# A hybrid decoder trunk: columns of layer 1's modulation on VectorE, head 1's queries and keys in the gates' banks, sums of activations behind the last exchange of banks

## The chip, the cores and the metric

The kernel runs on one core of one Trainium2 chip. The time is that of the device, in microseconds, from the start of the program to its end. Three runs of the kernel before gave 2206.76, 2210.25 and 2211.48; the median is 2210.25. A core has five engines that follow their own queues of instructions and wait for each other by semaphores: TensorE (PE: matrix products; its loads of weights are shown apart, as PEld), VectorE (DVE), ScalarE (ACT), GpSimd (POOL) and SyncE (SP), which here only issues transfers. Transfers between the large memory and the core's own memory are made by 16 DMA engines.

## The reference, cut to what matters

Two layers work on 512 tokens of width 2048 in 32-bit floats. The first is a multi-scale retention with 8 heads, the second a latent attention with 16 heads. Ahead of each, the activations are normalised and modulated by a conditioning vector c:

```python
c_act = jax.nn.silu(c)
for i in range(DEPTH):
    mod = (c_act @ ada_w[i] + ada_b[i])[:, None, :]
    shift, scale, gate = jnp.split(mod, 3, axis=-1)
    h = rmsnorm(x, norm_g[i]) * (1.0 + scale) + shift
    ...
    y = retention_branch(h, positions, ret_w_in[j], ret_gn_g[j], ret_w_out[j])
    ...
    x = x + gate * y
return rmsnorm(x, final_norm_g)
```

The retention branch first makes `h @ w_in`, which holds queries and keys, values and gates of all heads; then it turns queries and keys by the positions (rope), forms the retention per head, normalises, multiplies by `silu(g)` and goes through `w_out`. The change touches only the modulation of the first layer (called layer 1 in the title; index 0 in the code) and the projection `h @ w_in` for heads 0 and 1.

## The kernel before

**Numbers in two parts.** Each 32-bit operand of a product is split into a high part and a low part in TensorE's own rounded format (`split`, L135 and L136: ScalarE casts the high part, VectorE subtracts it to get the low one), and each product is made as three: high by high, high by low, low by high. A tile of h, `hT[kt]`, holds 128 of the 2048 features for all 512 tokens, high and low.

**The first stage: head 0 while h is made.** h is not complete when the kernel starts. Its 16 k-tiles are made two at a time (a unit `u` is the tiles 2u and 2u+1), and each unit is multiplied with head 0's weights as soon as it is there. For each tile two rows of the modulation are needed, the shift and the scale. `sum_mod` (L355) forms each as a sum over 2048 products on VectorE, in place on a loaded tile `aw` of 1 MB, and leaves one number per partition, `mc`. `make_first` (L365) turns the two into the column `b_col` (shift plus bias) and the column `a_col` ((scale + bias) times the gain of the norm), with two instructions on 128x1 elements on POOL (L368, L369). `make_h` (L243, L245) then makes h on ScalarE, once rounded as the high part and once in full as `h_<kt>f`, and VectorE subtracts the two for the low part (L246). The `aw` tiles have four buffers, which is one unit's worth.

Head 0 has three sets of four results: queries and keys (`qk`), values (`v`) and gates (`g`). The accumulator memory has eight banks, four under the tag `acc` and four under `aux`. The gates keep `aux` for the whole stage. `qk` and `v` share `acc` in turn: `swap` copies the four banks of one out to ordinary memory (L381) and those of the other back in (L385), pair by pair, on ScalarE. In unit u one of the two is `here` and one `there`; the products of a unit come in the order here, gates, exchange, there, and the next unit's `here` is the same kind, so that one exchange per unit is enough. `prepare_ahead(u + 1)` puts the work for the next unit ahead of these products: the split of the new `here` weights, the sums of the modulation, the normalisation of the next x tiles (`xT`, L541), h of tile 2u+2, and the splits of gate and `there` weights. `prepare_behind` puts h of tile 2u+3 behind the exchange.

**The end of the stage.** In the last unit, behind h of tile 15, two of eight groups of sums of activations are formed (`form_sums`, L441 to L446 and the split of their results; they are operands of the seven-product scheme that the later heads use for values and gates), then the tables of cosines and sines (`rotary_tables`, L257 to L280: a load of the positions on ScalarE's queue, 17 steps on VectorE, two on ScalarE). The last products of `here` and of the gates follow; then the values are copied out and stored (POOL issues the stores), `qk` comes back for its last 24 products, and the tables are stored.

**Head 1 and on.** The work of the later heads is a list of steps; each step loads weights three ahead, splits them one step ahead and multiplies. Head h makes its queries and keys in 8 steps of 24 products into four `acc` banks (L161 to L163), then values and gates in 16 steps by seven products instead of eight (L745 to L747), into x and s (banks `acc`) and z and y (banks `aux`). Between the stage above and the first step stands the evacuation of head 0: four copies of `qk` (`keep_rows`, L653) and four of the gates with Silu, each followed by a store that POOL issues. The remaining six groups of sums are formed in the first steps of head 1.

**What sets the order.** `queued` and `behind` fix the order per engine: what is emitted under them comes, on ScalarE, VectorE, TensorE and SP, behind the last instruction emitted there so far. An engine works through its queue in order. POOL is not among these four; its instructions come in the order of the scheduler. Tiles come from rings of buffers (six for `tmp`, from which h in full, the positions, the copies on their way to a store and the sums all take one), and a tile waits until the buffer that it takes is free.

Of the kernel before, what the change touches and what calls it, by code (L numbers as in the profile page):

```python
# [12 lines left out]
AF = mybir.ActivationFunctionType  # L13
ALU = mybir.AluOpType
AX = mybir.AxisListType

P = 128
# [32 lines left out]
def hybrid_trunk_kernel(  # L50
# [26 lines left out]
    PE, ACT, DVE, POOL = nc.tensor, nc.scalar, nc.vector, nc.gpsimd  # L77
# [11 lines left out]
    g_d = dram.tile([RH * T, T], F32, name="g_d")  # L89
# [5 lines left out]
    def big(name, dt=F32R):  # L95
        return base.tile([P, 2, T], dt, tag="big", bufs=16, name=name)
# [7 lines left out]
    def tmp(name, shape=(P, T)):  # L104
        return base.tile(list(shape), F32, tag="tmp", bufs=6, name=name)
# [95 lines left out]
    def w_block(w, ki, b):  # L201
        return w[0][:, ki, b * P : (b + 1) * P], w[1][:, ki, b * P : (b + 1) * P]
# [4 lines left out]
    def act_row(t):  # L207
        return t[:, 0, :], t[:, 1, :]
# [8 lines left out]
    bias_c = (vcol[:, 0:32], vcol[:, 32:64])  # L217
    norm_c = (vcol[:, 64:80], vcol[:, 80:96])
# [5 lines left out]
    a_col = [base.tile([P, KD], F32, name=f"a_col{i}") for i in range(2)]  # L224
    b_col = [base.tile([P, KD], F32, name=f"b_col{i}") for i in range(2)]
# [14 lines left out]
    def make_h(i, kt, src, dst):  # L240

        sc, bi = a_col[i][:, kt : kt + 1], b_col[i][:, kt : kt + 1]
        ACT.activation(dst[:, 0, :], src, AF.Identity, bias=bi, scale=sc)  # L243
        hf = tmp(f"h{i}_{kt}f")
        ACT.activation(hf, src, AF.Identity, bias=bi, scale=sc)  # L245
        return lambda: DVE.tensor_sub(dst[:, 1, :], hf, dst[:, 0, :].bitcast(F32))  # L246
# [51 lines left out]
    def qk_parts(h, u):  # L298
        return [
            (lambda raw: raw[:, :, 0:256], rows(w_ret_in, u, 2, h * 256, 256)),  # L300
            (lambda raw: raw[:, :, 256:512], rows(w_ret_in, u, 2, 2048 + h * 256, 256)),
        ]

    hT = [None] * KD
# [10 lines left out]
    banks = {}  # L315
# [31 lines left out]
    mods = {}  # L347
# [17 lines left out]
    def make_first(kt):  # L365

        k1 = slice(kt, kt + 1)
        POOL.tensor_add(b_col[0][:, k1], mods[kt, 0], bias_c[0][:, k1])  # L368
        POOL.tensor_scalar(  # L369
            out=a_col[0][:, k1], in0=mods[kt, 1], scalar1=bias1[:, k1], scalar2=norm_c[0][:, k1], op0=ALU.add, op1=ALU.mult  # L370
        )
        hT[kt] = big(f"hT_{kt}")
        return make_h(0, kt, xT[kt // 2][:, kt % 2, :], hT[kt])
# [38 lines left out]
    @contextmanager  # L412
    def behind(*engines):

        with ExitStack() as stack:
            for e in engines:
                ins = next((i for i in reversed(nc.cur_bb.bb.instructions) if i.engine == e), None)
                if ins is not None:
                    stack.enter_context(tc.issue_after(ins))
            yield  # L420

    def queued(fn, *args):
        with behind(A_, V_, T_, S_):
            return fn(*args)
# [59 lines left out]
    bias1 = l0p.tile([P, KD], F32, name="bias1")  # L484
# [58 lines left out]
    def load_unit(u):  # L543
        here, there = ("qk", "v") if u % 2 == 0 else ("v", "qk")
        load_first(here, u)
        load_mods(2 * u)
        if u > 1:
            queued(nc.sync.dma_start, xT[u], x_t[u])
        load_first("g", u)
        mods[2 * u + 1, 0] = queued(load_mod, 2 * u + 1, 0)  # L550
        load_first(there, u)
        mods[2 * u + 1, 1] = queued(load_mod, 2 * u + 1, 1)

    late = {}
    sums1 = {}
# [5 lines left out]
    def prepare_ahead(u, first=None):  # L561


        here, there = ("qk", "v") if u % 2 == 0 else ("v", "qk")
        low = queued(prepares[here, u])
        queued(sum_mod, 2 * u, 0)
        if first is not None:
            queued(first)
        queued(low)
        if u > 1:  # L570
            queued(normalise, u)
        queued(sum_mod, 2 * u, 1)
        low = queued(make_first, 2 * u)
        queued(sum_mod, 2 * u + 1, 0)
        queued(low)
        low = queued(prepares["g", u])
        late[u] = queued(prepares[there, u])
        queued(low)
        queued(sum_mod, 2 * u + 1, 1)

    def prepare_behind(u):

        low = queued(make_first, 2 * u + 1)
        queued(late[u])
        return low
# [26 lines left out]
    for u in range(1, NU):  # L612

        here, there = ("qk", "v") if u % 2 == 0 else ("v", "qk")
        more = u + 1 < NU
        if more:
            load_unit(u + 1)
            prepare_ahead(u + 1, low)
        else:
            queued(low)  # L620
            for n in range(2):
                queued(form_sums, n, hT, sums1, staged0, None)
            for _ in range(8):
                queued(next, tables)
        for kt in (2 * u, 2 * u + 1):
            queued(products, here, kt)
        for kt in (2 * u, 2 * u + 1):
            queued(products, "g", kt)
        if more:
            queued(swap, here, there)  # L630
            low = prepare_behind(u + 1)
        else:
            for b, ps in enumerate(banks["v"]):
                st = tmp(f"v0_st{b}")
                queued(ACT.copy, st, ps)
                POOL.dma_start(v_d[b * P : (b + 1) * P, :], st)
            queued(swap, None, "qk")
            for _ in tables:
                pass
            for n, t in enumerate(ret_tables):  # L640
                POOL.dma_start(tables_d[n * P : (n + 1) * P, :], t)
        queued(bank_products, there, u)
    qk0, g0 = banks["qk"], banks["g"]
    l0.__exit__(None, None, None)


# [215 lines left out]
    def qk_parts_of(h):  # L862
        return lambda u: qk_parts(h, u)
# [5 lines left out]
    for h in range(1, RH):  # L869
        if h < 6:  # L870
            steps += plain_steps(
                8, 2, qk_parts_of(h), 512, f"qk{h}", acc, 4,
                lambda w, ki, kt, b: w_block(w, ki, b), lambda w, ki, kt, b: act_row(hT[kt]),
                lambda b, ps, h=h: keep_rows(ps, qk_d, (4 * h + b) * P, f"qk{h}_st{b}", own=in_turn(b)),
                rows=lambda u, h=h: int(h > 1),
                sums=lambda u, h=h: {0: 2, 1: 3, 3: 4, 4: 5, 6: 6, 7: 7}.get(u) if h == 1 else None,
            )
        steps += heads_steps(h)
# [235 lines left out]
    for h in (6, 7):  # L1114
# [3 lines left out]
            lambda b, ps, h=h: keep_rows(  # L1118
                ps, qk_d, (4 * h + b) * P, f"qk{h}_st{b}",
                own=tmp,  # L1120
            ),
# [785 lines left out]
    n_prepared = prepare_for(0)  # L1907
    for b in range(4):
        queued(keep_rows, qk0[b], qk_d, b * P, f"qk0_st{b}", AF.Identity, in_turn(b))
    for b in range(4):  # L1910
        queued(keep_rows, g0[b], g_d, b * P, f"g0_st{b}", AF.Silu, tmp)
    for i, step in enumerate(steps):
        if i == n_p:
            lp.__exit__(None, None, None)
# [271 lines left out]
```

## Time and profile before

| what | value |
|---|---|
| median of three runs | 2210.25 us (2206.76 to 2211.48) |
| the profiled execution's own time | 2210.5 us |
| its span, first to last instruction | 2208.7 us |
| mean granted clock of TensorE | 0.992 |
| instructions | 27660 |
| busy share PE, DVE, ACT, POOL | 98%, 71%, 46%, 6% |
| chain of waits, by engine | PE 80%, DVE 8%, issue 4%, ACT 3%, DMA 3%, POOL 1% |
| moved from and to the large memory | 443.41 MB, 201 GB/s in the mean |

The profile records one execution. Start times count from the start of the span. A row of a group or of a timeline gives the line of the kernel, the engine, the operation, the tile written and the tiles read, and at its end in brackets the idle time of the engine ahead of it and what ended that. The chain of waits is followed back from the last instruction of a stretch: at each step to what released it. "issue" is time in it for which the profile shows no cause. A window sums busy time per engine between two instants and gives the granted clock (1.00 is full speed), the share of the DMA engines and the rate. TensorE's products overlap, so that busy time counts a little more than their spacing.

### The profile page before, as it was taken

How to read it: one execution, taken by the hardware profiler on the slowest of the kernel's cores; microseconds unless marked ns; L12 is line 12 of the kernel's file. 1: busy time of each engine (PE TensorE's matmuls, PEld its weight loads, DVE VectorE, ACT ScalarE, POOL GpSimd, SP SyncE). 2: the span in 40 equal slices, each digit the busy share in tenths (PEclk: the TensorE clock that was granted, in tenths of full speed). 3: DMA queues.
4: the chain of work that ended last, by engine and by line, in shares of the span. 5: the costliest groups of instructions: out<-in, count | busy, mean ns of one | idle time of the engine just before them, and what ended most of it. 6: DMA issues, size and time to landing. Idle time of an engine off the chain costs nothing.

```text
span 2208.7 us, 27660 instructions
## 1 busy us (share of the span) xinstructions
PE 2159.7 (98%) x10192; PEld 1802.5 (82%) x10192; DVE 1560.8 (71%) x2317; ACT 1006.0 (46%) x1516; POOL 140.7 (6%) x210
## 2 busy tenths in 40 slices
PE   7888999999999999999999999999999999999997
PEld 5777888888888877888888888888888888898887
DVE  7777866767675798866676776658877667776545
ACT  5554443434343444434343535434444266664443
POOL 1321000000100000000000000000000000000000
PEclk9999999999999999999999999999999999999999
DMA  9974686676867688673555556444457733235333
GB/s 382 358 257 147 191 281 224 225 257 195 280 200 267 209 281 270 219 242 127 208 201 166 203 164 219 157 157 129 143 196 281 286 96 94 77 114 172 119 105 133
DMA packets 205691, 443.41 MB, mean 201 GB/s; under 512 B 19393, under 2 KB 56289, under 8 KB 201713
## 3 DMA queue, kind: packets, MB, share of 16 engines
q1 hardware_dynamic: 193344, 402.45, 54.6%
q0 software_dynamic: 11920, 38.91, 4.5%
q8 instruction: 80, 1.31, 0.3%
q14 instruction: 57, 0.47, 0.1%
q10 hardware_dynamic: 290, 0.27, 0.0%
HBM read 398.56 MB, written 43.00 MB: 200 GB/s over the span
## 4 chain that ended last, share of the span: by engine, by line
PE 80%; DVE 8%; issue 4%; ACT 3%; DMA 3%; POOL 1%; SPq 0%; DVEq 0%; POOLq 0%; ACTq 0%
PE o L1196 13%; PE qk L161 4%; PE qk L162 4%; PE qk L163 4%; PE o L2052 4%; PE x L746 2%; PE y L746 2%; PE y L747 2%; PE y L745 2%; PE x L747 2%; PE s L746 2%; PE s L747 2%; PE x L745 2%; PE s L745 2%; PE o L163 2%
## 5 line engine op out<-in xcount | busy, mean ns | idle before, releaser
L1196 PE MATMUL o<-o_h,o_whi 128*128 128x512 f32 (+1 forms) x496 | 192.2, 388 | 0.0
L1196 PE MATMUL o<-o_h,o_wlo 128*128 128x512 f32 (+1 forms) x496 | 191.4, 386 | 0.0
L1196 PE MATMUL o<-o_l,o_whi 128*128 128x512 f32 (+1 forms) x496 | 191.3, 386 | 0.0
L161 PE MATMUL qk<-hT,qk_h 128*128 128x512 f32 x448 | 175.7, 392 | 5.7 <-ACT qk_st L653 5.7
L162 PE MATMUL qk<-hT,qk_h 128*128 128x512 f32 x448 | 175.3, 391 | 0.0
L163 PE MATMUL qk<-hT,qk_l 128*128 128x512 f32 x448 | 175.3, 391 | 0.0
L136 DVE TENSOR_TENSOR o_wlo<-o_r,o_whi 128x1024 fp32r<-128x1024 f32 x61 | 74.6, 1223 | 80.9 <-ACT o_whi L135 80.9
L136 DVE TENSOR_TENSOR qk_l<-qk_r,qk_h 128x1024 fp32r<-128x1024 f32 x56 | 68.1, 1223 | 68.5 <-ACT qk_h L135 68.2
L1196 PEld LDWEIGHTS o<-o_h,o_wlo 128*128 128x128 f32 x496 | 93.2, 188 | 18.9
L1196 PEld LDWEIGHTS o<-o_h,o_whi 128*128 128x128 f32 x496 | 93.2, 188 | 18.2
L1196 PEld LDWEIGHTS o<-o_l,o_whi 128*128 128x128 f32 x496 | 93.2, 188 | 18.2
L161 PEld LDWEIGHTS qk<-hT,qk_h 128*128 128x128 f32 x448 | 84.8, 189 | 23.7 <-ACT qk_st L653 6.1
L163 PEld LDWEIGHTS qk<-hT,qk_l 128*128 128x128 f32 x448 | 84.6, 189 | 17.9 <-DVE qk_l L136 0.3
L162 PEld LDWEIGHTS qk<-hT,qk_h 128*128 128x128 f32 x448 | 84.7, 189 | 17.6
L135 ACT CAST qk_h<-qk_r 128x1024 fp32r<-128x1024 f32 x56 | 57.9, 1050 | 85.9 <-PE qk L162 66.5
L898 DVE SCALAR_TENSOR_TENSOR mod<-mod,c_bm 128x1024 f32<-128x1024 f32 x64 | 78.0, 1219 | 20.5 <-DMA mod<-in_ada_t_dram 20.5
L161 PE MATMUL g<-h,g_h 128*128 128x512 f32 x232 | 90.6, 390 | 0.3 <-ACT g_h L135 0.3
L162 PE MATMUL g<-h,g_h 128*128 128x512 f32 x232 | 90.3, 389 | 0.0
L163 PE MATMUL g<-h,g_l 128*128 128x512 f32 x232 | 89.8, 389 | 0.0
L355 DVE SCALAR_TENSOR_TENSOR aw<-aw,c_all 128x2048 f32<-128x2048 f32 (+1 forms) x34 | 72.9, 2160 | 3.6 <-DMA aw<-in_ada_t_dram 3.1
L135 ACT CAST o_whi<-o_r 128x1024 fp32r<-128x1024 f32 x61 | 63.5, 1052 | 20.2 <-issue 10.0
L136 DVE TENSOR_TENSOR o_w_lo<-o_w_raw,o_w_hi 128x1024 fp32r<-128x1024 f32 x32 | 39.0, 1220 | 36.9 <-ACT o_w_hi L135 36.8
(1259 smaller groups left out, 6039.8 us busy)
## 6 DMA issues: line engine op xcount, KB each, us to landing
mod<-in_ada_t_dram SPq DMA_DIRECT2D x128, 512.0 KB, 6.0
o_r<-in_ret_w_out_dram SPq DMA_DIRECT2D x64, 512.0 KB, 4.3
aw<-in_ada_t_dram SPq DMA_DIRECT2D x30, 1024.0 KB, 8.8
qk_r<-in_ret_w_in_dram SPq DMA_DIRECT2D x112, 256.0 KB, 4.1
g_r<-in_mla_w_in_dram SPq DMA_DIRECT2D x32, 512.0 KB, 4.6
o_w_raw<-in_mla_w_out_dram SPq DMA_DIRECT2D x32, 512.0 KB, 3.7
qk_d<-qk_st POOLq DMA_DIRECT2D x32, 256.0 KB, 3.5
qk_r<-qk_d SPq DMA_DIRECT2D x32, 256.0 KB, 5.9
```

The source lines that it names most:

```text
L135: ACT.copy(hi, src)
L136: DVE.tensor_sub(lo, src, hi.bitcast(F32))
L161: PE.matmul(o, lhs[0], rhs[0], start=first and not seeded, stop=False, skip_group_check=seeded)
L162: PE.matmul(o, lhs[0], rhs[1], start=False, stop=False, skip_group_check=seeded)
L163: return PE.matmul(o, lhs[1], rhs[0], start=False, stop=last, skip_group_check=seeded)
L355: DVE.scalar_tensor_tensor(out=aw[:, cols], in0=aw[:, cols], scalar=1.0, in1=c_all[:, cols], op0=ALU.mult, op1=ALU.mult, accum_out=col[:, ...
L745: PE.matmul(banks[b], a[0], w[0], start=first, stop=False, skip_group_check=True)
L746: PE.matmul(banks[b], a[0], w[1], start=False, stop=False, skip_group_check=True)
L747: PE.matmul(banks[b], a[1], w[0], start=False, stop=True, skip_group_check=True)
L898: DVE.scalar_tensor_tensor(out=aw, in0=aw, scalar=1.0, in1=silu_c[j], op0=ALU.mult, op1=ALU.mult, accum_out=mc[:, j, b : b + 1],)
L1196: PE.matmul(o, w[i][:, ki, c0 + b * P : c0 + (b + 1) * P], a[j], start=first and i + j == 0, stop=last and i == 1, skip_group_check=True,)
L2052: PE.matmul(banks2[b][:, cols], w[0][i][:, 0, b * P : (b + 1) * P], o2_moving(w, u, cols)[j], start=u + i + j == 0, stop=u == KD - 1 and i ...
```

## The change

It has three parts. The two columns of `make_first` are formed on VectorE: the addition stays an addition, and the other becomes one instruction with two inputs and a scalar. Head 1's queries and keys take the `aux` banks, which the gates of head 0 held, instead of `acc`. And at the end of the first stage the order is another: the first two groups of sums move from behind h of tile 15 to behind the last exchange of banks and the tables; the gates of head 0 are copied out and stored there, ahead of the sums, instead of behind the queries and keys of head 0.

```diff
@@ make_first
-        POOL.tensor_add(b_col[0][:, k1], mods[kt, 0], bias_c[0][:, k1])
-        POOL.tensor_scalar(
-            out=a_col[0][:, k1], in0=mods[kt, 1], scalar1=bias1[:, k1], scalar2=norm_c[0][:, k1], op0=ALU.add, op1=ALU.mult
+        DVE.tensor_add(b_col[0][:, k1], mods[kt, 0], bias_c[0][:, k1])
+        DVE.scalar_tensor_tensor(
+            out=a_col[0][:, k1], in0=mods[kt, 1], scalar=bias1[:, k1], in1=norm_c[0][:, k1], op0=ALU.add, op1=ALU.mult
         )
@@ the last unit, behind h of tile 15
             queued(low)
-            for n in range(2):
-                queued(form_sums, n, hT, sums1, staged0, None)
             for _ in range(8):
                 queued(next, tables)
@@ the last unit, behind the exchange
             for n, t in enumerate(ret_tables):
                 POOL.dma_start(tables_d[n * P : (n + 1) * P, :], t)
+            for b, ps in enumerate(banks["g"]):
+                st = tmp(f"g0_st{b}")
+                queued(ACT.activation, st, ps, AF.Silu)
+                POOL.dma_start(g_d[b * P : (b + 1) * P, :], st)
+            for n in range(2):
+                queued(form_sums, n, hT, sums1, staged0, None)
         queued(bank_products, there, u)
-    qk0, g0 = banks["qk"], banks["g"]
+    qk0 = banks["qk"]
@@ the steps of queries and keys
-                8, 2, qk_parts_of(h), 512, f"qk{h}", acc, 4,
+                8, 2, qk_parts_of(h), 512, f"qk{h}", aux if h == 1 else acc, 4,
@@ ahead of the loop over the steps
     for b in range(4):
         queued(keep_rows, qk0[b], qk_d, b * P, f"qk0_st{b}", AF.Identity, in_turn(b))
-    for b in range(4):
-        queued(keep_rows, g0[b], g_d, b * P, f"g0_st{b}", AF.Silu, tmp)
```

Three places show how instructions move. The first is VectorE in the middle of the first stage, around h of tile 8 (`aw_0` and `aw_1` are the loaded rows of shift and scale, `mc` their sums; lines with + are new):

```order
 L541 TENSOR_TENSOR xT_209<-xT_209,x_factors 128x1024
 L355 SCALAR_TENSOR_TENSOR aw_1_720,mc_1_739<-aw_1_720,c_all 128x2048
+L368 TENSOR_TENSOR b_col_90<-mc_0_734,vcol 128x1
+L369 SCALAR_TENSOR_TENSOR a_col_88<-mc_1_739,bias_140,vcol 128x1
 L355 SCALAR_TENSOR_TENSOR aw_0_725,mc_0_747<-aw_0_725,c_all 128x2048
 L246 TENSOR_TENSOR hT_743<-h_8f,hT_743 128x512
 L334 TENSOR_TENSOR g_4_k4b_751<-g_4_raw,g_4_k4b_750 128x1024
 L355 SCALAR_TENSOR_TENSOR aw_1_729,mc_1_757<-aw_1_729,c_all 128x2048
+L368 TENSOR_TENSOR b_col_90<-mc_0_747,vcol 128x1
+L369 SCALAR_TENSOR_TENSOR a_col_88<-mc_1_757,bias_140,vcol 128x1
 L334 TENSOR_TENSOR v_4_wlo_754<-v_4_raw,v_4_whi_753 128x1024
```

Each pair now stands in VectorE's queue right behind the second of its two sums; POOL's queue loses the same 32 instructions.

The second is ScalarE from h of tile 15 to the first weights of head 1, before (`qk_0_h` is the high part of head 1's first weights, `qk_24_0` a bank of head 0's queries and keys, `g_0` one of its gates):

```order
L245 ACTIVATE h_15f<-xT_212,b_col_90,a_col_88 128x512
L135 CAST sums_1281<-sums_f 128x2x256
...
L254 DMA ret_pi<-in_positions_dram 128x512
...
L279 ACTIVATE ret_sin<-ret_sin 128x512
L280 ACTIVATE ret_cos<-ret_cos,rt 128x512
L135 CAST qk_0_h<-qk_0_r 128x1024
L653 ACTIVATE qk_st_1435<-qk_24_0_1381 128x512
...
L653 ACTIVATE g_st_1447<-g_0_305 128x512
```

The same with the change:

```order
L245 ACTIVATE h_15f<-xT_212,b_col_90,a_col_88 128x512
L254 DMA ret_pi<-in_positions_dram 128x512
...
L279 ACTIVATE ret_sin<-ret_sin 128x512
L280 ACTIVATE ret_cos<-ret_cos,rt 128x512
L424 ACTIVATE g_st_1363<-g_0_305 128x512
...
L135 CAST sums_1384<-sums_f 128x2x256
...
L135 CAST qk_0_h<-qk_0_r 128x1024
L657 ACTIVATE qk_st_1447<-qk_24_0_1351 128x512
```

The load of the positions follows h at once; four gate copies and four casts of sums now stand ahead of the cast of head 1's weights. On VectorE the sums stand likewise between the last step of the tables and the low part of these weights.

The third is TensorE where head 1's queries and keys end and its values and gates begin, before:

```order
L163 MATMUL qk_3_1469<-hT_1242,qk_7_l 128x512
L745 MATMUL z_0_1842<-vg_00o_h,hT_335 128x512
L746 MATMUL z_0_1842<-vg_00o_l,hT_335 128x512
L747 MATMUL z_0_1842<-vg_00o_h,hT_335 128x512
L745 MATMUL x_0_1838<-vg_00e_h,hT_271 128x512
```

and with the change:

```order
L163 MATMUL qk_3_1469<-hT_1242,qk_7_l 128x512
L749 MATMUL x_0_1838<-vg_00e_h,hT_271 128x512
L750 MATMUL x_0_1838<-vg_00e_l,hT_271 128x512
L751 MATMUL x_0_1838<-vg_00e_h,hT_271 128x512
L749 MATMUL x_1_1839<-vg_00e_h,hT_271 128x512
```

The first three products of z (a bank that was free while queries and keys held `acc`) no longer come first; x and s do, whose banks are now free.

## The prediction

> **What bounds the kernel now.** I read the page first (shares, slices), then the chain of waits, then windows cut at the places where the chain shows a repeat, and last the timelines of single engines inside one repeat.
>
> ```profile
> PE 2159.7 (98%) x10192; PEld 1802.5 (82%) x10192; DVE 1560.8 (71%) x2317; ACT 1006.0 (46%) x1516; POOL 140.7 (6%) x210
> ```
>
> TensorE is busy for 98% of the span, so little can be won by faster work elsewhere, except where TensorE is idle or slow. One such stretch is the first 190 us, which the change touches. There each unit of two k-tiles costs 72 products: 24 of queries and keys, 24 of values, 24 of gates. I cut the windows at the first product behind each exchange of banks; the columns are time, busy time and instruction count of PE, PEld, DVE, ACT, POOL, granted clock, DMA share, GB/s.
>
> ```profile
> 44.41:62.84 18.43, 15.61 (x60) 11.96 (x60) 15.89 (x15) 10.46 (x16) 4.46 (x4) 0.91 1.02 411
> 62.84:81.80 18.96, 16.62 (x73) 13.44 (x73) 14.95 (x15) 10.49 (x16) 5.98 (x4) 1.00 1.00 381
> 81.80:101.89 20.09, 18.26 (x73) 14.59 (x73) 14.95 (x15) 10.59 (x16) 5.97 (x4) 0.92 0.83 321
> 101.89:121.96 20.07, 18.24 (x73) 14.59 (x73) 14.95 (x15) 10.59 (x16) 5.98 (x4) 0.91 0.86 307
> 121.96:140.91 18.95, 16.63 (x72) 13.43 (x73) 14.95 (x15) 10.47 (x16) 5.98 (x4) 1.00 0.89 338
> 140.91:160.93 20.02, 18.20 (x72) 14.62 (x72) 14.95 (x15) 10.59 (x16) 5.97 (x4) 0.92 0.52 187
> 178.99:190.30 11.31, 5.61 (x26) 4.32 (x24) 8.66 (x15) 2.67 (x4) 1.08 (x2) 0.93 0.11 42
> 200.00:220.00 20.00, 20.00 (x90) 16.57 (x89) 18.34 (x31) 8.94 (x13) 0.00 (x0) 1.00 0.48 151
> ```
>
> The five full repeats last 19.0 to 20.1 us. No engine fills one: TensorE has 16.6 us of work at full clock, VectorE 14.95, ScalarE 10.5. So a loop of dependences sets the period, and the chain of waits spells it out for the repeat that ran at clock 1.00 (start, length, what):
>
> ```profile
> 121.03 2.30 DVE aw L355 x2
> ...
> 123.43 3.38 POOL a_col L369
> ...
> 127.55 0.80 ACT h_11f L245
> 128.35 0.95 ACT qk_whi L332
> ...
> 130.47 1.22 DVE xT L541
> 131.69 2.22 DVE aw L355 x2
> ...
> 134.00 2.32 POOL a_col L369
> ...
> 137.07 0.80 ACT h_12f L245
> 137.88 0.94 ACT g_k4b L332
> 138.81 0.94 ACT v_whi L332
> ...
> 140.27 0.60 ACT qk L385
> ...
> 140.91 0.79 PE qk L398
> ```
>
> POOL's 128x1 operation stands in that loop twice, for 5.7 of 18.95 us. Its length is not its work. The timelines of POOL and VectorE show one beside an idle VectorE and one beside a busy one:
>
> ```profile
> 32.83 0.34 POOL L369 TENSOR_SCALAR a_col<-mc,bias,vcol 128x1 f32<-128x1 f32 x1 [4.54 <-DVE aw L355]
> 94.79 2.29 DVE L355 SCALAR_TENSOR_TENSOR aw<-aw,c_all 128x2048 f32<-128x2048 f32 x1
> 94.98 2.31 POOL L369 TENSOR_SCALAR a_col<-mc,bias,vcol 128x1 f32<-128x1 f32 x1 [8.20 <-DVE aw L355]
> ...
> 55.79 2.46 POOL L369 TENSOR_SCALAR a_col<-mc,bias,vcol 128x1 f32<-128x1 f32 x1 [4.54 <-DVE aw L355]
> ```
>
> The first took 0.34 us alone; the second 2.31 us, with a long sum on VectorE, ending just behind it. POOL gets its turn only when VectorE's next instruction is over, and ScalarE's h waits for that.
>
> **Part 1, the columns on VectorE.** 32 small POOL instructions go, 32 come on VectorE, each pair right behind the sum that it needs. Nearest row for their length, and the row that tells what else holds ScalarE at the odd tile:
>
> ```profile
> 21.15 0.16 DVE L361 TENSOR_TENSOR mc_0b<-mc 128x1 f32<-128x1 f32 x1
> 125.04 0.59 ACT L385 COPY v<-part_v 128x512 f32<-128x512 f32 x1
> ```
>
> One costs 0.16 us; a pair, overlapped as neighbours on VectorE are, about 0.3 until ScalarE may start. Even tile: the sum ends at 133.91, so h starts at 134.3 where POOL let it start at 136.35: 2.05 us. Odd tile: ScalarE itself is in the exchange until 125.63, so h starts there instead of 126.83: 1.2 us. The loop falls from 18.95 to 15.7. VectorE gains two pairs, some 0.4 us of its own time: 15.4 of work. They wait for nothing but the sum in front of them; what stands behind them there (the next sum, or the low half of the other kind's weights) moves by 0.2 us. Even if a small instruction cost double, 0.32, the loop would be 16.0.
>
> TensorE's 72 products are then the longest: 16.4 us (16.63 busy counts the fill of the last product twice; 72 at the spacing of the last window, 20.00 us for some 88, give 16.4). So the period becomes 16.4, TensorE does not wait for an exchange, and with no gap I take the clock as 1.00, as in 200 to 220. The bounds of a period are 16.3 and 20.1, today's.
>
> Loads must keep up: a unit moves 338 GB/s x 18.95 us = 6.4 MB (307 x 20.07 gives 6.2); at 6.3 MB, the 411 GB/s of the first window needs 15.3 us, the 338 of a later one 18.6. I take 411: there the engines were full (1.02), later they had nothing asked of them (0.89).
>
> ```profile
> aw<-in_ada_t_dram SPq DMA_DIRECT2D x18, 1024.0 KB, 7.8
> ```
>
> A column load lands 7.8 us after its issue; in a 16.4 us period the sum that frees a buffer lies 11 us or more ahead of the next use.
>
> Up to the first of these windows the loads are late and little changes. The exchange at its end follows h of tile 4, whose column took 2.46 us on POOL (the row at 55.79) and should take 0.3: the product at 62.84 comes at 60.7. Five periods of 16.4 put the product now at 160.93 to 142.7: **18.2 us gained**, the main term.
>
> **Part 2, the order behind the last tile.** The chain of waits of this place, then single rows that price the moved work:
>
> ```profile
> 165.35 0.72 ACT h_15f L245
> ...
> 173.93 3.20 DMA ret_pi<-in_positions_dram
> ...
> 186.85 0.70 DVE ret_cos L277
> ...
> 188.82 0.93 ACT qk_h L135
> ...
> 190.30 0.79 PE qk L161
> ```
>
> ```profile
> 166.70 1.29 DVE L441 TENSOR_TENSOR h_f<-hT 128x512 f32<-128x512 f32 x2
> 171.01 1.28 DVE L441 TENSOR_TENSOR h_f<-hT 128x512 f32<-128x512 f32 x2
> 193.24 2.09 ACT L653 ACTIVATE g_st<-g 128x512 f32<-128x512 f32 x4
> 189.11 0.54 POOL L641 DMA_DIRECT2D tables_d<-ret_cos  x1
> v_d<-v_st POOLq DMA_DIRECT2D x4, 256.0 KB, 3.2
> ```
>
> From the end of h_15f (166.05) to the first product of head 1 (190.30) are 24.25 us, of which TensorE is idle for the last 5.7. Two sums of 4.31 us each came first, and the load of the positions, on ScalarE's queue, was issued behind their casts. Now this load is issued right behind h_15f, the tables follow, and the sums come behind them, ahead of the split of head 1's first weights on both engines. SP's queue keeps its order.
>
> With h_15f ending at 147.7 (5.0 behind 142.7; it was 5.12 behind 160.93, with a POOL wait of 1.2 partly in it): load 3.2, tables 10.4 (177.13 to 187.55), so the tables end at T = 161.4. ScalarE then has sine and cosine (1.27, from 187.55 to 188.82) and four gates (2.0): it is free for casts at T+3.3, some 0.7 later than the first sums could use it, so these end at T+5.0. The second sums take the buffer of a gate: its copy ends at T+1.8, POOL's issues (three of 0.54, two for the tables) end at T+2.65, landing near T+5.5 at 3.2 us. They take 4.31, and their last cast ends some 0.8 before their last low half: T+9.05; head 1's high part ends at T+10.0, the first product runs at T+10.05 = 171.5. Its low part follows 1.3 us later, which costs the third product 0.25 us. From h_15f to there are 24.05 us: **0.2 us gained**, a draw. TensorE's stall stays, about 7 us where it was 5.7, because what it waits for moved from the emptying of head 0's banks to the sums. If the store lands only after 7.8 us, like the column loads, the part costs 4.6 more; if it never matters, 0.5 less.
>
> **Part 3, head 1 in the gates' banks.** The four gate copies move ahead of head 1 (priced above, they lie beside the sums on VectorE). At the end of head 1's queries and keys, x and s no longer wait for ScalarE:
>
> ```profile
> 236.84 0.39 PE L747 MATMUL z<-vg_00o_h,hT 128*128 128x512 f32 x1
> 237.33 0.50 PE L745 MATMUL x<-vg_00e_h,hT 128*128 128x512 f32 x1
> ```
>
> Products are 0.23 apart, so 0.26 us was lost; z and y, which wait now, come 2.8 us later, behind the copies. **0.26 us gained.** On POOL's queue the four gate stores pass the four of head 0's queries and keys, 0.54 us each; the only one of these that anything here waits for is priced above.
>
> **Sum.** 18.2 + 0.1 (offset of h_15f) + 0.2 + 0.26 = 18.8 us. The profiled execution took 2210.5 (span 2208.7), 0.25 above the median of the runs: 2210.5 - 18.8 = 2191.7. Behind 260 us TensorE is never idle for long and no stage is tied to the clock on the wall, so the gain stays.
>
> **Rivals.** *The clock keeps falling.* In four of six windows the clock was 0.91 or 0.92 and the same products took 18.2 us. If gaps are not the cause, the period is 18.2: the last exchange comes at 60.7 + 91 = 151.7, gain 9.2 + 0.6, time 2200.7. Against it: 1.00 in 200 to 220, where TensorE never waits. The Trainium skill, "TensorE: Matmul & The Clock Gate", section "What's actually happening", has the clock halve after an idle window of about 3.4 us. By that rule the gaps here (18.95 less 16.63, so 2.3) are too short to halve it, and this rival would hold; the rows leave it open, for gaps of this size stand ahead of windows at 0.91 and of one at 1.00.
>
> *The loads bind.* At 338 GB/s the period is 18.6, the last exchange at 153.7, gain 7.2 + 0.6, time 2202.7. For it: the engines are full until 81.8. Against: 411 GB/s was reached. The Trainium skill, "DMA: Bandwidth & Descriptors", section "Where 436 GB/s comes from", gives about 358 GB/s as a core's share of HBM. By that figure, an estimate, a unit takes 17.6 us and the time is 2197.7; the window at 411 speaks against it.
>
> *Slower: the tail is exposed.* The positions are now fetched just as head 1's first weights are: three loads of 0.52 MB, 3.8 us at 411 GB/s, ahead of them; with the late store (4.6) the first product of head 1 comes 8.4 us later than in my sum. That decides only if the first stage gains under 8 us; with no gain there, because h waits for its column loads as soon as POOL is gone, the time is 2210.5 + 8.4 - 0.5 = 2218.4.
>
> *It was hidden anyway.* The loop has another member that I missed, the period stays near 19: within 4 us of before, near 2208.
>
> **How the numbers follow.** My forecast has 0.66, the clock 0.10, the loads 0.12, hidden 0.07, slower 0.05. What a measurement of this kernel can tell from no change is about 0.2%, 4.4 us. The first three lie beyond it: faster 0.88, same 0.07, slower 0.05. The predicted time is the forecast's, 2192. Downward the range takes a period of 16.3, a first exchange 2 us earlier and the 4.7 us between the lowest and highest run: 2185. Upward it takes in both rivals on the same side: 2203.
>
> **What would show it.** Right: windows of 16.3 to 16.7 us between exchanges from 60 us on, with PE idle near zero and clock 1.00; no POOL rows at L369; the first product of head 1 near 171 with one wait of about 7 us ahead, ended by the split of its weights; x before z with no gap. Wrong: waits of VectorE for column loads (rival 2), clock 0.91 in windows without gaps (rival 1), a period still near 19 (hidden), or more than 28 us between h_15f and head 1 (slower).

## The result, and the profile after

| | before | with the change |
|---|---|---|
| median of four runs each | 2209.84 us (2206.76 to 2211.48) | 2189.03 us (2188.32 to 2189.77) |
| profiled execution, span | 2208.7 us | 2187.2 us |
| mean granted clock | 0.992 | 0.995 |
| first product of the last exchange | 160.93 us | 142.34 us |
| first product of head 1 | 190.30 us | 169.28 us |

The ratio is 0.9907 (95% interval 0.989 to 0.9925): 20.8 us faster, 3 us better than forecast. Of the 21.5 us between the two spans 18.6 were won by the last exchange, 2.4 more by the first product of head 1, and 0.5 behind it.

The page's line of busy times, with the change: POOL has lost its 32 instructions, VectorE has them.

```profile
PE 2151.8 (98%) x10192; PEld 1798.2 (82%) x10192; DVE 1564.2 (72%) x2349; ACT 1005.8 (46%) x1516; POOL 101.2 (5%) x178
```

The windows between the first products behind the exchanges, columns as in the prediction:

```profile
43.94:60.67 16.73, 15.94 (x60) 12.17 (x61) 16.51 (x20) 10.90 (x16) 0.00 (x0) 0.90 1.03 413
60.67:77.00 16.33, 16.33 (x74) 13.50 (x72) 15.12 (x19) 10.34 (x16) 0.00 (x0) 1.00 1.03 402
77.00:93.32 16.32, 16.32 (x73) 13.49 (x73) 15.27 (x19) 10.53 (x16) 0.00 (x0) 1.00 1.02 413
93.32:109.67 16.35, 16.35 (x73) 13.50 (x73) 15.29 (x19) 10.54 (x16) 0.00 (x0) 1.00 1.03 403
109.67:126.01 16.34, 16.34 (x73) 13.49 (x73) 15.27 (x19) 10.54 (x16) 0.00 (x0) 1.00 1.02 406
126.01:142.34 16.33, 16.33 (x74) 13.50 (x74) 15.29 (x19) 10.55 (x16) 0.00 (x0) 1.00 0.71 263
```

From 60.67 on TensorE is busy for the whole of every window, at clock 1.00. The five full periods take 16.3 us where they took 19.0 to 20.1. The DMA engines were as good as full up to 126 us (share 1.02 to 1.03, 402 to 413 GB/s) and still on time. The chain of waits around one exchange is now TensorE alone:

```profile
83.97 4.08 PE v L398 x18
88.05 5.44 PE g L398 x24
93.49 7.73 PE qk L398 x34
```

The timelines of VectorE and ScalarE in the same stretch show what took the place of POOL's 2.3 to 3.4 us:

```profile
88.22 0.15 DVE L368 TENSOR_TENSOR b_col<-mc,vcol 128x1 f32<-128x1 f32 x1
88.34 0.22 DVE L369 SCALAR_TENSOR_TENSOR a_col<-mc,bias,vcol 128x1 f32<-128x1 f32 x1
88.59 0.82 ACT L243 ACTIVATE hT<-xT,b_col,a_col 128x512 fp32r<-128x512 f32 x1 [4.89 <-DVE a_col L369]
...
98.98 1.05 ACT L332 CAST v_whi<-v_raw 128x1024 fp32r<-128x1024 f32 x1 [0.69 <-PE qk L398]
```

h starts 0.3 us after its sum. The last row matters below: this split of weights waits 0.69 us for TensorE, which still reads the buffer.

The end of the stage, from the timelines of several engines (an ACTq row is the issue of a transfer on ScalarE's queue):

```profile
145.27 0.36 ACTq L254 DMA_DIRECT2D ret_pi<-in_positions_dram  x1
146.50 0.80 ACT L245 ACTIVATE h_15f<-xT,b_col,a_col 128x512 f32<-128x512 f32 x1
149.32 0.43 DVE L257 CAST ret_sin<-ret_pi 128x512 f32<-128x512 int32 x1 [1.29 <-DMA ret_pi<-in_positions_dram]
159.02 0.69 DVE L277 SCALAR_TENSOR_TENSOR ret_cos<-ret_sin 128x512 f32<-128x512 f32 x1
...
160.90 2.04 ACT L424 ACTIVATE g_st<-g 128x512 f32<-128x512 f32 x4
167.14 1.14 ACT L135 CAST sums<-sums_f 128x512 fp32r<-128x512 f32 x2 [3.17 <-DVE sums_f L444]
168.18 1.04 ACT L135 CAST qk_h<-qk_r 128x1024 fp32r<-128x1024 f32 x1
169.28 0.62 PE L161 MATMUL qk<-hT,qk_h 128*128 128x512 f32 x1 [5.00 <-ACT qk_h L135]
170.54 0.79 PE L163 MATMUL qk<-hT,qk_l 128*128 128x512 f32 x1 [0.21 <-DVE qk_l L136]
```

From the end of h of tile 15 (147.30) to head 1 are 21.98 us, 24.25 before. The stall is there as forecast, ended by the split of head 1's weights, but it is 5.0 us and not 7. It is paid in clock too: in the 20 us from head 1's first product on (169.28 to 189.28) the granted clock is 0.91, some 1.8 us of TensorE's time; before, from 190.30 on, it was 0.87. The load of the positions was issued at 145.27, while ScalarE had h of tile 15 still before it.

### The profile page after: what moved, and what is told of

It reads as the page before. It is cut to its first block, busy times and chain, and to the rows that moved or that the text cites. A ratio compares the mean times of both kernels' runs of the same rounds, so it can differ in the third digit from the quotient of the medians.

```text
span 2187.2 us, 27642 instructions
## 1 busy us (share of the span) xinstructions
PE 2151.8 (98%) x10192; PEld 1798.2 (82%) x10192; DVE 1564.2 (72%) x2349; ACT 1005.8 (46%) x1516; POOL 101.2 (5%) x178
## 4 chain that ended last, share of the span: by engine, by line
PE 84%; DVE 7%; issue 4%; ACT 3%; DMA 2%; POOL 0%; SPq 0%; DVEq 0%; POOLq 0%; ACTq 0%
PE o L1200 13%; PE qk L163 4%; PE qk L161 4%; PE qk L162 4%; PE o L2054 4%; PE x L750 2%; PE y L750 2%; PE y L751 2%; PE y L749 2%; PE x L751 2%; PE s L750 2%; PE s L751 2%; PE x L749 2%; PE s L749 2%; PE o L162 2%
## 5 line engine op out<-in xcount | busy, mean ns | idle before, releaser
L1200 PEld LDWEIGHTS o<-o_h,o_wlo 128*128 128x128 f32 x496 | 93.2, 188 | 18.8
L1200 PEld LDWEIGHTS o<-o_l,o_whi 128*128 128x128 f32 x496 | 93.2, 188 | 18.2
L163 PEld LDWEIGHTS qk<-hT,qk_l 128*128 128x128 f32 x448 | 84.4, 188 | 18.6 <-DVE qk_l L136 0.9
L902 DVE SCALAR_TENSOR_TENSOR mod<-mod,c_bm 128x1024 f32<-128x1024 f32 x64 | 78.1, 1221 | 21.5 <-DMA mod<-in_ada_t_dram 21.4
```

The source lines that it names most:

```text
L163: return PE.matmul(o, lhs[1], rhs[0], start=False, stop=last, skip_group_check=seeded)
L902: DVE.scalar_tensor_tensor(out=aw, in0=aw, scalar=1.0, in1=silu_c[j], op0=ALU.mult, op1=ALU.mult, accum_out=mc[:, j, b : b + 1],)
L1200: PE.matmul(o, w[i][:, ki, c0 + b * P : c0 + (b + 1) * P], a[j], start=first and i + j == 0, stop=last and i == 1, skip_group_check=True,)
```

## The experiments

The theory at the start: the columns carry nearly all; POOL's instruction is held while VectorE works and h waits for it; without that wait TensorE has no gap and keeps its clock. In the edits, lines with - are those of the kernel with the change, lines with + those of the run; ... stands for lines left out. Rivals: the gain comes from the other two parts; it is a matter of POOL's own work; the clock has a cause of its own.

**The columns alone.** Parts 2 and 3 undone:

```diff
             queued(low)
+            for n in range(2):
+                queued(form_sums, n, hT, sums1, staged0, None)
             for _ in range(8):
...
-            for b, ps in enumerate(banks["g"]):
-                st = tmp(f"g0_st{b}")
-                queued(ACT.activation, st, ps, AF.Silu)
-                POOL.dma_start(g_d[b * P : (b + 1) * P, :], st)
-            for n in range(2):
-                queued(form_sums, n, hT, sums1, staged0, None)
...
-                8, 2, qk_parts_of(h), 512, f"qk{h}", aux if h == 1 else acc, 4,
+                8, 2, qk_parts_of(h), 512, f"qk{h}", acc, 4,
...
+    for b in range(4):
+        queued(keep_rows, g0[b], g_d, b * P, f"g0_st{b}", AF.Silu, tmp)
```

> Part 1 alone: the columns of layer 1's modulation on VectorE, all else as before. My theory (the columns on POOL held the loop of the first stage; with them on VectorE TensorE sets the period): five periods of 16.3 to 16.4 us without gaps, the last exchange's first product near 142.5 us, h_15f near 147.3, and then the old order of the end with its 24.25 us, so that head 1 starts near 171.6 and the time is 2209.8 - 18.7 = 2191. Rival (most of the gain comes from the new order at the end, the columns bring little): 2203 or more, periods near 19.

Measured: 2191.42 us (2190.68 to 2191.62), ratio 0.9915 (0.9901 to 0.9928). The columns give 18.6 us and the other two parts 2.4. Its timeline of TensorE shows where these come from:

```profile
172.14 0.79 PE L161 MATMUL qk<-hT,qk_h 128*128 128x512 f32 x1 [7.54 <-ACT qk_st L653]
```

With a faster first stage the old order stalls for 7.5 us instead of 5.7.

**Parts 2 and 3 alone**, with both small instructions back on POOL:

```diff
-        DVE.tensor_add(b_col[0][:, k1], mods[kt, 0], bias_c[0][:, k1])
-        DVE.scalar_tensor_tensor(
-            out=a_col[0][:, k1], in0=mods[kt, 1], scalar=bias1[:, k1], in1=norm_c[0][:, k1], op0=ALU.add, op1=ALU.mult
+        POOL.tensor_add(b_col[0][:, k1], mods[kt, 0], bias_c[0][:, k1])
+        POOL.tensor_scalar(
+            out=a_col[0][:, k1], in0=mods[kt, 1], scalar1=bias1[:, k1], scalar2=norm_c[0][:, k1], op0=ALU.add, op1=ALU.mult
```

> Parts 2 and 3 alone: the new order at the end and head 1's queries and keys in the gates' banks, the columns still on POOL. My theory: periods stay at 19 to 20 us, the end gains the 2.3 us that the changed kernel showed between h_15f and head 1 (21.98 for 24.25) and 0.26 at head 1's x: 2209.8 - 2.6 = 2207.2. Rival (the order is the gain): 2195 or less.

Measured: 2209.08 us (2205.14 to 2211.33), the kernel before beside it 2210.0, ratio 0.9996 (0.9987 to 1.0005). No large gain, so the rival is out; the 2.6 us expected lie at the edge of the interval, and the time does not settle them. The rows of this kernel:

```profile
162.06 0.50 PE L398 MATMUL v<-v_whi,hT 128*128 128x512 f32 x1 [1.83 <-ACT v L385]
166.39 0.80 ACT L245 ACTIVATE h_15f<-xT,b_col,a_col 128x512 f32<-128x512 f32 x1
189.24 0.80 PE L161 MATMUL qk<-hT,qk_h 128*128 128x512 f32 x1 [5.10 <-ACT qk_h L135]
```

From h of tile 15 (167.19) to head 1 it takes 22.05 us, 2.2 less than before. But in this execution the last exchange came 1.1 us later than in the one of before, because one more of the later periods ran at clock 0.91. While the gaps are there, which periods lose clock varies, and a gain of 2 us drowns in it: runs of before spread over 4.7 us, runs of the change over 1.5.

**The columns on VectorE, but later.** Those of the even tiles behind the next sum instead of in front of it:

```diff
-        low = queued(make_first, 2 * u)
         queued(sum_mod, 2 * u + 1, 0)
+        low = queued(make_first, 2 * u)
```

> The changed kernel, but the columns of each even tile from tile 2 on stand in VectorE's queue behind the next sum instead of ahead of it, so that they come 2.2 us later, about when POOL used to deliver them; POOL has none of this work. My theory (what counts is when the column comes, not which engine makes it): loop 15.7 + 2.2 = 17.9, 1.5 us more in each of some 5 or 6 periods, with gaps at the exchanges; if the clock falls in some of these windows as before, 1 us more each: 2189 + 8 to 14 = 2197 to 2203. Rival (POOL's instructions disturbed VectorE or ScalarE, and their absence is the gain): 2189, periods of 16.3.

Measured: 2211.05 us (2208.82 to 2212.63), ratio 1.0001 (0.9992 to 1.001). The whole gain is gone, so what counts is when h gets its column, not which engine makes it. My number was too low, though: a delay of one sum cost 22 us. One window and one row of ScalarE:

```profile
85.48:105.55 20.07, 18.24 (x73) 14.59 (x73) 15.41 (x19) 10.52 (x16) 0.00 (x0) 0.91 0.88 334
```

```profile
100.99 0.82 ACT L243 ACTIVATE hT<-xT,b_col,a_col 128x512 fp32r<-128x512 f32 x1 [7.05 <-DVE a_col L369]
```

h waits 2.2 us longer (7.05 for 4.89), the period grows by 3.7. The clock has come down too. The next three runs take this apart.

**Gaps of a chosen length.** The copy-out of the first bank is made three, four or five times in each exchange, which is 0.62 us more on ScalarE for each copy, and nothing else (the 3 becomes 4 and 5):

```diff
-                ACT.copy(keep, ps)
+                for _ in range(3 if b == 0 else 1):
+                    ACT.copy(keep, ps)
```

> The change, with the copy-out of the first bank made three times in each exchange: two copies of 0.6 us more on ScalarE, 1.2 us. The exchange then comes some 1.0 us after TensorE has run out of products (0.2 us of slack now). Theory one (a gap costs its own length and also lowers the granted clock behind it): period 17.4 at clock 1.00 plus up to 1.7 where the clock falls to 0.92, 19 in all, seven periods, 2205 to 2209. Theory two (a gap of 1 us costs only itself): period 17.4, clock 1.00, 2195 to 2197. Theory three (the slack was larger than it looks): 2189 to 2191.

> The change, with the copy-out of the first bank made four times in each exchange: three copies of 0.62 us more on ScalarE. With two more copies the gap was 0.91 us, the period 17.53 and the clock 1.00; now the gap should be 1.5 and the period 18.15. Theory one (the clock falls behind gaps as long as those of the kernel before, 1.8 us, and not behind 1.5): clock 1.00, seven periods of 1.8 more, 2201 to 2203. Theory two (it falls behind any gap over 1 us): clock 0.92 in most periods, 1.2 to 1.7 more in each, 2209 to 2214.

> The change, with the copy-out of the first bank made five times in each exchange: four copies of 0.62 us more. The gap should be 2.1 us and the period 18.8 at clock 1.00. Theory one (the gap is what lowers the clock, as in the kernel before): clock 0.91 to 0.92 in most periods, these take 20 to 20.3, and the time is 2211 to 2216 though only 17 us of copies were added. Theory two (the lower clock of the kernel before had another cause): clock 1.00, 2206 to 2207.

Measured: 2196.09 us (2195.51 to 2199.89), 2202.46 us (2201.44 to 2202.6) and 2213.78 us (2211.54 to 2216.0). Windows and TensorE's row with the gap, of the kernel with two copies more, then three, then four:

```profile
80.38:97.91 17.53, 16.61 (x73) 13.44 (x73) 15.28 (x19) 11.71 (x18) 0.00 (x0) 1.00 0.98 379
```

```profile
97.91 0.50 PE L399 MATMUL qk<-hT,qk_whi 128*128 128x512 f32 x1 [0.92 <-ACT qk L386]
```

```profile
81.32:99.48 18.16, 16.63 (x72) 13.43 (x72) 15.26 (x19) 12.29 (x19) 0.00 (x0) 1.00 0.95 366
```

```profile
99.48 0.50 PE L399 MATMUL qk<-hT,qk_whi 128*128 128x512 f32 x1 [1.53 <-ACT qk L386]
```

```profile
85.84:106.24 20.40, 18.25 (x72) 14.57 (x73) 15.28 (x19) 12.87 (x20) 0.00 (x0) 0.92 0.87 337
```

```profile
106.24 0.50 PE L399 MATMUL qk<-hT,qk_whi 128*128 128x512 f32 x1 [2.15 <-ACT qk L386]
```

Gaps of 0.9 and 1.5 us lengthen the period by 1.2 and 1.8 us and no more, and the clock stays at 1.00 in all five full periods of each kernel. Gaps of 2.15 bring it to 0.92 in all five, which adds 1.6 us to each (18.25 busy for 16.62). The 0.92 is a mean. Cut finer, the windows of the last kernel show the clock at one half, and soon back:

```profile
107.00:108.00 1.00, 1.00 (x4) 0.81 (x3) 1.00 (x1) 0.97 (x2) 0.00 (x0) 0.50 1.08 410
111.00:112.00 1.00, 1.00 (x6) 0.82 (x5) 0.61 (x1) 0.36 (x1) 0.00 (x0) 1.00 0.84 327
```

From the gap's end at 106.24 to 112 the clock is at 0.50 for 3.4 us in all, which loses half of that, 1.7 us. So the longer gap is what brings the lower clock here, and the last step, 0.62 us of copies, lengthens the period by 2.2 us (20.40 for 18.16).

The first of these runs also measures the slack that the change leaves. Two copies are 1.24 us, the period grew by 1.20: there was next to none. The loop of dependences is then 17.53 - 1.24 = 16.29 us long. Its chain of waits goes through TensorE: the 24 products behind an exchange have to end before the split of the next weights can start. Two rows of this chain, and the same products in the chain of the late columns, where the clock had fallen:

```profile
80.38 5.75 PE v L399 x24
...
86.15 1.06 ACT qk_whi L332
```

```profile
85.48 7.37 PE v L398 x24
```

With this the late columns come out as well: 16.29, and 2.16 later, and 1.6 of clock make 20.05, where 20.07 was measured.

**The same work on POOL, with nobody waiting.** Both small instructions are made on VectorE as in the change, and a second time on POOL into a place that is not read:

```diff
+        POOL.tensor_add(probe[:, 0, k1], mods[kt, 0], bias_c[0][:, k1])
+        POOL.tensor_scalar(
+            out=probe[:, 1, k1], in0=mods[kt, 1], scalar1=bias1[:, k1], scalar2=norm_c[0][:, k1], op0=ALU.add, op1=ALU.mult
+        )
```

> The change, with both small instructions of every tile done a second time on POOL, into a place that nobody reads. Theory (POOL's instruction is held while VectorE's long one runs, and only who waits for it pays): POOL's rows of 128x1 last 2.3 to 3.4 us again in the middle of the stage, the period stays 16.3 to 16.4 and the time 2189 (2188 to 2190). Rival (POOL's instruction also costs VectorE time, 0.3 us or more each): the period becomes 17 or more, TensorE waits at the exchanges, 2193 or more.

Measured: 2188.95 us (2187.88 to 2191.07), as the change. POOL and VectorE in one place of it:

```profile
78.48 3.54 POOL L374 TENSOR_SCALAR probe<-mc,bias,vcol 128x1 f32<-128x1 f32 x1 [2.27 <-DVE b_col L369]
```

```profile
78.54 1.22 DVE L334 TENSOR_TENSOR qk_wlo<-qk_raw,qk_whi 128x1024 fp32r<-128x1024 f32 x1
79.68 2.28 DVE L356 SCALAR_TENSOR_TENSOR aw<-aw,c_all 128x2048 f32<-128x2048 f32 x1
```

POOL's instruction on one element per partition is held from 78.48 to 82.02, through two instructions of VectorE, and ends just behind the second; VectorE's take as long as without it. The long rows on POOL were a wait, and only who stands behind that wait pays.

**The sums back ahead of the tables**, the gates' copies and banks kept:

```diff
             queued(low)
+            for n in range(2):
+                queued(form_sums, n, hT, sums1, staged0, None)
             for _ in range(8):
                 queued(next, tables)
...
-            for n in range(2):
-                queued(form_sums, n, hT, sums1, staged0, None)
```

> The change, with the first two groups of sums back ahead of the tables (the gates' copies and banks stay as in the change). Theory (the order of sums and tables carries the gain at the end of the first stage: the positions are fetched while VectorE is still at h of tile 15): the load of the positions is again behind the casts of the sums, 11.1 us from the end of h of tile 15 to the first step of the tables as in the kernel before; tables 10.4, sine and cosine 1.3, gate copies 2.0, split 1.0: head 1 starts at 147.3 + 25.8 = 173.1 instead of 169.28, and the time is 2189.0 + 3.9 = 2192.9, above the kernel with the columns alone (2191.4). Rival (the early gate copies and the other banks carry it): 2189 to 2190.

Measured: 2192.69 us (2192.19 to 2194.03), ratio 0.9924 (0.991 to 0.9937). Two rows of it:

```profile
155.37 0.36 ACTq L254 DMA_DIRECT2D ret_pi<-in_positions_dram  x1
```

```profile
173.45 0.79 PE L161 MATMUL qk<-hT,qk_h 128*128 128x512 f32 x1 [9.00 <-ACT qk_h L135]
```

The order is worth 3.7 us. The early gate copies without it cost 1.3 (2192.69 against the columns' 2191.42), since they then stand ahead of the split that TensorE waits for. Together they make the 2.4.

**Getting rid of the stall.** All eight groups of sums in head 1's eight steps, none ahead of head 1:

```diff
-            for n in range(2):
-                queued(form_sums, n, hT, sums1, staged0, None)
...
-                sums=lambda u, h=h: {0: 2, 1: 3, 3: 4, 4: 5, 6: 6, 7: 7}.get(u) if h == 1 else None,
+                sums=lambda u, h=h: u if h == 1 else None,
```

> The changed kernel, but all eight groups of sums are formed in head 1's steps, one per step, behind the split of the next weights; none stands ahead of head 1's first split. My theory (the 5.0 us stall ahead of head 1 is the wait for a split that stands behind the sums): ScalarE is free behind the gates near 162.9, the high part is ready near 164, TensorE ends the first stage at 164.3: the stall falls from 5.0 to under 1 us. VectorE has some 5.5 us of work per step of 5.45, which its lead covers: 2189 - 4.5 = 2184.5. Rival (the sums are only moved: VectorE falls behind in head 1's steps and TensorE waits there instead): 2188 to 2190.

Measured: 2187.94 us (2187.02 to 2188.49), ratio 0.99 (0.9886 to 0.9913), 1.1 better than the change where 4.5 were expected. Head 1 starts 5.3 us earlier, without a stall (163.97), but TensorE's waits in this kernel have three new rows (us in total, times, the longest):

```profile
PE z L747 <- ACT qk_st L655: 2.5, 1, 2.5
...
PE x L748 <- DVE vg_00e_l L779: 0.9, 1, 0.9
...
PE qk L163 <- DVE qk_l L136: 0.5, 1, 0.5
```

Eight groups of 4.3 us and the low halves fill VectorE to the end of head 1's queries and keys; the eighth group holds ScalarE until 214.7, and with it the copies that free the banks for z. The window of that stretch has VectorE at 23.3 of 25 us:

```profile
190.00:215.00 25.00, 21.90 (x95) 17.24 (x93) 23.27 (x40) 8.81 (x13) 0.00 (x0) 1.00 0.45 147
```

So the stall was moved: TensorE waits 3.9 us in these three places.

**One group beside the tables, seven in the steps.** `form_sums` is cut into its additions and its split. The additions of the first group stand behind the tables, its split behind that of head 1's first weights:

```diff
-            for n in range(2):
-                queued(form_sums, n, hT, sums1, staged0, None)
...
-                sums=lambda u, h=h: {0: 2, 1: 3, 3: 4, 4: 5, 6: 6, 7: 7}.get(u) if h == 1 else None,
+                sums=lambda u, h=h: {u: u + 1 for u in range(7)}.get(u) if h == 1 else None,
...
+    f0 = queued(add_sums, 0, hT, staged1)
     n_prepared = prepare_for(0)
+    queued(split_sums, 0, sums1, f0, more1)
```

> The change, with one group of sums in VectorE's idle time behind the tables (its additions stand ahead of the split of head 1's first weights, its own split behind it) and the other seven in head 1's first seven steps, none in the eighth. Theory (with eight groups in eight steps VectorE was full, and the 2.5 us and 0.9 us that TensorE waited at the start of head 1's values and gates were the eighth group's): these waits go, head 1 starts without a stall, 2187.9 - 3.4 = 2184.5. Rival (VectorE falls behind all the same in seven full steps, and the wait stays): 2187 to 2188.

Measured: 2185.59 us (2184.14 to 2186.33), ratio 0.989 (0.9877 to 0.9904): 3.4 better than the change, 1.1 short of the theory. The wait for z is gone. A wait for the low half of head 1's first weights remains; TensorE's row and VectorE's:

```profile
167.06 0.50 PE L163 MATMUL qk<-hT,qk_l 128*128 128x512 f32 x1 [1.96 <-DVE qk_l L136]
```

```profile
164.31 0.42 DVE L446 TENSOR_TENSOR sums_f<-h_f 128x256 f32<-128x256 f32 x1 [2.96 <-ACT qk_h L135]
```

The additions themselves stopped for 3 us in the middle, and the low half stood behind them. Why their target tile was not free earlier was not followed up.

**The same group in VectorE's idle time ahead of the tables** (the other seven groups stay in head 1's steps), where it waited for h of tile 15 (2.2 us) and for the positions (1.3 us); the first step of the tables, which issues their load, stands ahead of it:

```diff
-            queued(low)
-            for _ in range(8):
+            queued(next, tables)
+            f0 = queued(add_sums, 0, hT, staged0)
+            queued(low)
+            queued(split_sums, 0, sums1, f0, None)
+            for _ in range(7):
                 queued(next, tables)
```

> As the kernel with one group of sums behind the tables and seven in head 1's steps, but this one group stands where VectorE waited for h of tile 15 (2.2 us) and for the positions (1.6 us); the load of the positions is issued ahead of it. Theory (of its 4.3 us 3.8 are hidden there, and the 2.0 us that TensorE waited for the low part of head 1's first weights shrink to 0.5 or 1.0): 2184 to 2185. Rival (the tables end later by the whole group, and all behind them): 2187 or more.

Measured: 2183.85 us (2182.48 to 2184.53), ratio 0.9879 (0.9864 to 0.9893): 5.2 us better than the change and the fastest of all. Head 1 starts at 164.66, 4.6 us earlier, and the 20 us behind that run at clock 1.00 instead of 0.91. TensorE's waits around head 1 are down to two rows:

```profile
165.91 0.50 PE L163 MATMUL qk<-hT,qk_l 128*128 128x512 f32 x1 [0.53 <-DVE qk_l L136]
...
210.65 0.50 PE L757 MATMUL x<-vg_00e_l,hT 128*128 128x512 f32 x1 [0.87 <-DVE vg_00e_l L788]
```

## Why the prediction was right, and where not

- **The period: right.** 16.3 us was forecast at 16.4, clock 1.00, no gap from 60.67 on. The main term is 18.6 (160.93 less 142.34) for 18.2; the columns alone gave as much in time.
- **Why the loop got shorter: right.** The late columns on VectorE took the gain back, POOL's work with nobody behind it cost nothing.
- **The loop itself: a member was missed.** I worked it out as 15.7 us, which would have left TensorE 0.7 us of slack; the run with two copies more shows 16.29 and next to none. The missing member is in the row at 98.98: the split of the next weights does not follow h at once but waits 0.69 us for TensorE to leave the buffer, and the chain of the run with two copies more has TensorE's 24 products in this place. It cost nothing, since TensorE's own 16.33 was still the longer, but only by 0.04 us, and that was luck. It also made my expectation for the late columns wrong: a loop that passes through TensorE grows by the lost clock as well (7.37 for 5.75, 1.6 us).
- **The clock: right, and now shown.** The rival that it falls without gaps is out: 1.00 in every window without one; the first window, at 0.90, stands behind a gap of 2.59 us. The other rival, the loads, is out as well: they ran at 402 to 413 GB/s where that rival had 338, and VectorE waited for them 2.3 us in all, as its group of long sums in the page of the change says:

```profile
L355 DVE SCALAR_TENSOR_TENSOR aw<-aw,c_all 128x2048 f32<-128x2048 f32 (+1 forms) x34 | 73.3, 2162 | 2.4 <-DMA aw<-in_ada_t_dram 2.3
```

- **The end of the stage: the term that was mis-sized.** I forecast 24.05 us from h of tile 15 to head 1, a gain of 0.2. In this, 0.25 was the wait of head 1's third product, so to its first product it was 23.8; measured are 21.98, a gain of 2.3. Of the 2.2 us by which head 1 came earlier than forecast (169.28 for 171.5), 0.4 is the earlier h. Another 1.3 is the load of the positions: I let it be issued behind h and take 3.2; it was issued 2.0 us before h ended, took 4.0, and the tables ended at 159.7 instead of 161.4. The last 0.5 is the gate's store: I let the second group of sums wait for it, and no such wait is in the trace. The prediction had named this 0.5 as the lower bound of that step.
- **Small terms:** the third product of head 1 waited 0.21 (0.25 forecast). x stands ahead of z without a gap. Behind the first product of head 1 the span is 0.5 shorter (0.26 forecast), but the clock there differs as well (0.91 for 0.87 in the first 20 us), which the prediction had not priced, so the 0.26 is not shown by itself.
- **The exposed tail**, the slower rival, did not come: its late store was the wait that isn't there.

Altogether 21.5 us came off the profiled execution where the sum had 18.8. Of the 2.7 between them, 2.1 lie between h of tile 15 and head 1, 0.4 ahead of the last exchange and 0.2 behind head 1's first product.

## What to carry to other kernels

A small instruction on an otherwise idle engine can stand on the critical loop for ten times its work, so compare its row beside a busy neighbour with its row alone before trusting that it is free. When TensorE's gaps are repeated, price them twice, by their length and by the clock that they may cost; bringing a gap to a length at which the clock holds (1.5 us here) is worth more than the same time elsewhere. And before work is moved out of a stall, add up the engine that takes it, step by step: the stall moved here until the idle stretches that were really there were used.

## What the runs showed of the hardware that was not expected

- **How long a gap of TensorE may be.** Gaps of 1.53 us, six in a row, left the clock at 1.00; gaps of 2.15 us, also six in a row, brought it to 0.92 every time. But the length alone does not decide. In the kernel before, these two gaps were followed by windows at 1.00, others of 1.83 and 2.33 by windows at 0.91 and 0.92:

```profile
62.84 0.50 PE L398 MATMUL qk<-hT,qk_whi 128*128 128x512 f32 x1 [2.32 <-ACT qk L385]
121.96 0.50 PE L398 MATMUL v<-v_whi,hT 128*128 128x512 f32 x1 [1.83 <-ACT v L385]
```

  Behind 2.85 us (the kernel with parts 2 and 3 alone, at 62.90) and behind the 2.54 us of the wait for z the clock stayed at 1.00 as well. What else decides is not shown.

  The Trainium skill, "TensorE: Matmul & The Clock Gate", section "What's actually happening", puts the fall behind an idle window of about 3.4 us; here 2.15 us was enough, and the measurement decides.
- **POOL is held through more than one instruction of VectorE:** 3.54 us, the length of two, for work of 0.34. The Trainium skill, "SBUF — State Buffer", section "SBUF: two separate sides", speaks of an exclusive lock on a port pair that the two engines share, held for a whole instruction. The end of POOL's row just behind VectorE's agrees with that; that it was not let in between two of them goes further.
- **A load issued on ScalarE's queue can go out ahead of work written in front of it:** with the change it went out 2.0 us before h, the instruction in front of it, ended. How far ahead it can go is not shown: in the kernel before it went out at 173.93, only 0.06 us before the start of the last cast in front of it, which had waited for VectorE.
- **Two instructions on 128x1 elements cost VectorE 0.15 and 0.22 us**, 0.29 from the end of the sum to the start of h.
